# Gate and up of the last FFN as seven block products, and RWKV's row-group pairs in alternating order

## The chip, the cores and the metric

The kernel runs on one core of one Trainium2 chip. The metric is the device time of one execution in microseconds (us). A core has five engines that each run their own queue in order: PE (matrix products, 128 x 128 array, results in PSUM), DVE (vector operations), ACT (activations and copies), POOL and SP (here above all the issue of DMAs). PSUM has eight banks; a tile of 128 x 512 float32 numbers fills one.

## The reference

A trunk of two layers over 1024 tokens and 1024 features in float32, each layer a mixer and a SwiGLU FFN, with RMS norms before each and at the end. Layer 0 mixes with pooling and a Mamba-2 scan, layer 1 with RWKV-7 and RG-LRU.

```python
def swiglu(h, w_gate, w_up, w_down):
    return (jax.nn.silu(h @ w_gate) * (h @ w_up)) @ w_down

def reference(x, ...):
    h = x
    for layer in range(2):
        hn = rmsnorm(h, mix_norm_g[layer])
        mix = even_mixer(hn, ...) if layer % 2 == 0 else odd_mixer(hn, ...)
        h = h + mix
        hn = rmsnorm(h, ffn_norm_g[layer])
        h = h + swiglu(hn, ffn_w_gate[layer], ffn_w_up[layer], ffn_w_down[layer])
    return rmsnorm(h, final_norm_g)
```

`w_gate` and `w_up` are 1024 x 2816, `w_down` is 2816 x 1024. In RWKV-7 each of 8 heads has 64 channels, and two heads share the 128 rows of a tile.

## The kernel before, in words

The 1024 tokens are worked in two halves of 512 (`hf` 0 and 1, residuals `hA` and `hB`). Residuals lie transposed, features on the 128 partitions and 512 tokens along the free dimension, as 8 tiles. Float32 precision comes from splits: each operand is a high part (`hi`, an ACT cast to fp32r) and a low part (`lo`, DVE: source minus `hi`; `split`, lines 226 to 229, and for weights `wblock`, lines 341 and 342), and a product is three matmuls, high x high, high x low, low x high (`dense`, lines 363 to 365), each 128 rows deep with 512 moving columns.

An FFN half (`ffn`) takes F = 2816 as 22 blocks of 128, in 11 pairs. For a pair `gate_up` computes `pg` and `pu` (2 blocks x 8 k x 3 matmuls each), with tanh on ACT (line 493) and two products on DVE (494, 503) between; the result is split into `acth` and `actl`. Groups of pairs then go through `down`, four pairs of `py` tiles that are added into `h` (line 515). Of the last group in layer 1 `ffn_final` computes the down product with tokens on the partitions: `pf` holds the transposed residual (line 557) plus the products (lines 566 to 568, 256 columns); ACT squares and sums it (`fsq`, 570), a chain of small DVE operations gives the inverse root (`fst`, 572, 573, 214 to 218), and `xo` (577) is stored. `pg`, `pu`, `py` of `down`, and `pf` of the first two of four token tiles come from one pool of four PSUM banks (tag `pd`); the other four banks are a pool for everything else (`psum`).

The last FFN, `t.ffn(1, 1, hB, hn)`, follows the FFN of half 0 of the same layer, whose last pair calls `norm_apply` for `hB` beside it (line 297 on DVE, line 295 partly on POOL).

In the RWKV part `ps_A` (line 1156) are products of 64 rows: for each of 8 chunks and 4 head pairs, one matmul on the upper and one on the lower 64 rows of the array, into two PSUM tiles.

Weights are loaded into `raw` (3 buffers), their parts lie in `whi` and `wlo` (4 each). Other shared tags: `tf` (3), `sg` (2), `st` (3), `m` (28), `h` (8). The order of the instructions on each engine is set when the program is built, by a scheduler with its own simulation of time (`schedule_with_timeline_sim=True`); it keeps data dependencies and may otherwise mix work that the code issues one after the other. On the chip each engine keeps the order it was given.

Of the kernel before, what the change touches and what calls it, by code (L numbers as in the profile page):

```python
# [86 lines left out]
class Trunk:  # L87
# [453 lines left out]
    def ffn_final(self, hf, wd, base, act, h):  # L541

        nc = self.nc
        n = len(act)
        grep = [self.m2("grep") for _ in range(2)]
        for q in range(2):
            nc.sync.dma_start(grep[q], self.i["final_norm_g"][q * 512:(q + 1) * 512].rearrange("(o n) -> o n", o=1).broadcast_to([P, 512]))
        pair = lambda: [self.op.tile([P, 2, 256], F32R, name=x, tag="m", bufs=BUFS["m"]) for x in ("fh", "fl")]
        blk = []
        for m in range(4):  # L550
            blk.append(self.wblock(wd[base * P:(base + n) * P, m * 256:(m + 1) * 256], n, 256, pair))
        for c in range(4):
# [7 lines left out]
            for q in range(2):  # L560
                for k in range(n):
                    xh, xl = act[k]
                    for m in range(2):
                        wh, wl = blk[2 * q + m][k]
# [15 lines left out]
            self.tick()  # L580
            yield


# [324 lines left out]

    def odd_open(self, pool):
        nc, i = self.nc, self.i  # L910
        self.op = pool
        lng = pool.tile([P, H], F32, name="lng")
# [36 lines left out]
    def in1(self, hf, hn):  # L949
        nc, w = self.nc, self.i["od_w_in"][0]  # L950
        st = {}
# [5 lines left out]

        lw = self.op.tile([P, 2, 4, P], F32, name="lw", tag="m4", bufs=2)
        nc.gpsimd.memset(lw, 0.0)
# [89 lines left out]
    def rwkv(self, hf, st):  # L1049
        nc, op = self.nc, self.op  # L1050
        wdad, gd, r, k, v = st["wdad"], st["gd"], st["r"], st["k"], st["v"]
        TP = lambda n, shape, b=1: op.tile(shape, F32, name=n, tag=n, bufs=b)
        c64 = lambda a: a.rearrange("p (c t) -> p c t", c=8)
# [96 lines left out]
        for c in range(8):  # L1150
            am = op.tile([P, 4, 2, P], F32, name="am", tag="m4", bufs=2)
            pAs = [self.psum("ps_A") for _ in range(2)]
            for j in range(4):
# [11 lines left out]
        A = op.tile([P, 32, 32], F32, name="A", tag="m4", bufs=2)  # L1165
# [4 lines left out]
        X = op.tile([P, 32, 32], F32, name="X", tag="m4", bufs=2)  # L1170
        Xf = X.rearrange("p a b -> p (a b)")
# [20 lines left out]
        def prep1(c):  # L1192

            q, cc = c // 4, c % 4
            e = ch[c] = {}
            w1 = op.tile([P, 8, P], F32, name="w1", tag="m4", bufs=2)
            nc.sync.dma_start(w1, w1d[c])
# [124 lines left out]
    def gn(self, hf, c, y, v, bon, gd):  # L1322
# [6 lines left out]
        def part1():  # L1329
            s = op.tile([P, 4, 8], F32, name="gs", tag="gs", bufs=2)  # L1330
            mean, x, rs, t = (s[:, k, :] for k in range(4))
# [95 lines left out]
def trunk(tc, ins, out):  # L1427
    with ExitStack() as stack:
# [41 lines left out]
        t.later(2, lambda: rstd("B", stB))  # L1470
        with tc.tile_pool(name="op", bufs=1) as op:
            t.odd_open(op)
            hn2 = []
# [26 lines left out]
            t.flush()  # L1500
            run_all(t.ffn(1, 1, hB, hn))

# [27 lines left out]
```

## Time and profile before

| | |
|---|---|
| median of 3 runs | 2448.47 us (2446.02 to 2450.08) |
| profiled execution | 2448.01 us, of which the span of the trace is 2446.0 |
| PE busy | 2402.2 us (98%) |
| DVE busy | 1543.6 us (63%) |
| ACT busy | 911.6 us (37%) |
| POOL busy | 252.2 us (10%) |
| last FFN on PE | from 2065.3 us to the end |

Busy time counts each engine's instructions; a matmul's record is longer than the distance to the next one, since matmuls overlap, so the cost of one in a row is the distance between two starts, or the busy time of a window through the number of matmuls in it. The granted PE clock is given as a share of 2.4 GHz. A releaser in brackets is the instruction that ended the idle time before a row.

### The profile page before, as it was taken

Reading aid. Unit: us, or ns where it says so; the run is one execution under the profiler, and the core shown is the slowest. Engines: PE = TensorE matmul, PEld = TensorE weight load, DVE = VectorE, ACT = ScalarE, POOL = GpSimd, SP = SyncE. Lnnn points to the kernel's source line nnn. Section 1 sums busy time; section 2 is a strip of 40 time slices with the busy share of each in tenths; the row PEclk is TensorE's granted clock in tenths of the full one; section 3 lists DMA queues with packets and bytes.
Section 4 is the critical chain, followed back from the end, with each engine's and each line's share of the span. In section 5 each row is a group of like instructions: output and inputs, shape, how many; then the busy total and the mean of one; then the engine's idle time right before and its main releaser. Section 6 shows DMA issues by size and latency. Waiting matters only on the chain.

```text
span 2446.0 us, 33120 instructions
## 1 busy us (share of the span) xinstructions
PE 2402.2 (98%) x12323; PEld 1967.5 (80%) x12323; DVE 1543.6 (63%) x3052; ACT 911.6 (37%) x1612; POOL 252.2 (10%) x235
## 2 busy tenths in 40 slices
PE   7999999999999999999999999999999999999998
PEld 6878888888878887788888888877888888888887
DVE  7878767764476675675565768576465547444445
ACT  4434433222244564233333446432333334222222
POOL 2132121211111011100000110020000001000000
PEclk9989999999999999999999999999999999999999
DMA  5433533333345333543324533344432433333332
GB/s 164 119 90 102 161 107 109 90 113 95 92 152 158 89 106 95 162 143 106 97 80 138 168 112 104 96 136 137 138 101 81 142 121 125 96 95 95 95 95 78
DMA packets 296401, 280.17 MB, mean 115 GB/s; under 512 B 46130, under 2 KB 273608, under 8 KB 296240
## 3 DMA queue, kind: packets, MB, share of 16 engines
q1 hardware_dynamic: 295408, 277.64, 38.7%
q8 instruction: 97, 1.59, 0.3%
q0 software_dynamic: 832, 0.41, 0.1%
q14 instruction: 64, 0.52, 0.1%
HBM read 247.51 MB, written 30.49 MB: 114 GB/s over the span
## 4 chain that ended last, share of the span: by engine, by line
PE 91%; DVE 4%; DMA 2%; issue 1%; SPq 1%; ACT 1%; POOL 0%; DVEq 0%; ACTq 0%; POOLq 0%
PE pg L363 7%; PE pg L364 7%; PE pg L365 7%; PE pu L363 6%; PE pu L364 6%; PE pu L365 6%; PE py L363 6%; PE py L364 6%; PE py L365 6%; PE pi L363 5%; PE pi L364 5%; PE pi L365 5%; PE po L363 2%; PE po L364 2%; PE po L365 2%; PE ps_g L1259 1%
## 5 line engine op out<-in xcount | busy, mean ns | idle before, releaser
L342 DVE TENSOR_TENSOR wlo<-raw,whi 128x512 fp32r<-128x512 f32 (+1 forms) x744 | 538.5, 726 | 512.7 <-ACT whi L341 502.6
L341 ACT CAST whi<-raw 128x512 fp32r<-128x512 f32 (+1 forms) x744 | 458.8, 619 | 1050.9 <-PE pu L364 303.6
L363 PE MATMUL pu<-hnh,whi 128*128 128x512 f32 x736 | 292.5, 398 | 0.0
L365 PE MATMUL pu<-hnh,wlo 128*128 128x512 f32 x736 | 291.9, 397 | 0.0
L364 PE MATMUL pu<-hnl,whi 128*128 128x512 f32 x736 | 291.6, 396 | 0.0
L363 PE MATMUL pg<-hnh,whi 128*128 128x512 f32 x704 | 281.5, 400 | 0.0
L364 PE MATMUL pg<-hnl,whi 128*128 128x512 f32 x704 | 278.8, 396 | 0.0
L365 PE MATMUL pg<-hnh,wlo 128*128 128x512 f32 x704 | 276.5, 394 | 0.0
L363 PE MATMUL py<-acth,whi 128*128 128x512 f32 x672 | 262.8, 402 | 4.9 <-DVE sg L503 3.4
L364 PE MATMUL py<-actl,whi 128*128 128x512 f32 x672 | 266.7, 397 | 0.0
L365 PE MATMUL py<-acth,wlo 128*128 128x512 f32 x672 | 265.8, 396 | 0.0
L363 PE MATMUL pi<-hnh,whi 128*128 128x512 f32 x512 | 204.6, 400 | 0.2
L364 PE MATMUL pi<-hnl,whi 128*128 128x512 f32 x512 | 203.3, 397 | 0.0
L365 PE MATMUL pi<-hnh,wlo 128*128 128x512 f32 x512 | 201.7, 396 | 0.0
L363 PEld LDWEIGHTS pu<-hnh,whi 128*128 128x128 f32 x736 | 138.4, 188 | 33.4 <-issue 2.2
L365 PEld LDWEIGHTS pu<-hnh,wlo 128*128 128x128 f32 x736 | 138.4, 188 | 33.3 <-issue 0.7
L364 PEld LDWEIGHTS pu<-hnl,whi 128*128 128x128 f32 x736 | 138.4, 188 | 31.0
L363 PEld LDWEIGHTS pg<-hnh,whi 128*128 128x128 f32 x704 | 132.4, 188 | 30.9
L365 PEld LDWEIGHTS pg<-hnh,wlo 128*128 128x128 f32 x704 | 132.4, 188 | 30.8
L364 PEld LDWEIGHTS pg<-hnl,whi 128*128 128x128 f32 x704 | 132.3, 188 | 30.3
L363 PEld LDWEIGHTS py<-acth,whi 128*128 128x128 f32 x672 | 127.1, 189 | 36.8 <-issue 3.0
L365 PEld LDWEIGHTS py<-acth,wlo 128*128 128x128 f32 x672 | 127.0, 189 | 29.6
(443 smaller groups left out, 3737.0 us busy)
## 6 DMA issues: line engine op xcount, KB each, us to landing
raw<-in_ffn_w_gate SPq DMA_DIRECT2D x88, 512.0 KB
raw<-in_ffn_w_up SPq DMA_DIRECT2D x88, 512.0 KB
raw<-in_ffn_w_down SPq DMA_DIRECT2D x64, 512.0 KB
raw<-in_od_w_in SPq DMA_DIRECT2D x44, 512.0 KB
raw<-in_ev_w_in SPq DMA_DIRECT2D x36, 512.0 KB
raw<-in_ffn_w_down SPq DMA_DIRECT2D x48, 256.0 KB
yraw<-yd SPq DMA_DIRECT2D x32, 256.0 KB
raw<-in_ev_w_out SPq DMA_DIRECT2D x16, 512.0 KB
```

What stands on the lines that cost most here:

```text
L341: nc.scalar.copy(hi[:, :m, :width], raw[:, k:k + m, :width])
L342: nc.vector.tensor_tensor(lo[:, :m, :width], raw[:, k:k + m, :width], hi[:, :m, :width].bitcast(F32), op=SUB)
L363: nc.tensor.matmul(o, wh[:, a:b], xh, start=st, stop=False)
L364: nc.tensor.matmul(o, wh[:, a:b], xl, start=False, stop=False)
L365: nc.tensor.matmul(o, wl[:, a:b], xh, start=False, stop=en)
L1259: nc.tensor.matmul(pg[:, hs], e["w1"][:, h, :], e["S"][:, hs], start=h == 0, stop=h == 7)
```

## The change

The last FFN's gate and up products are replaced. For each block of 128 columns of F the two weight matrices and the two halves of the normalised input form a 2 x 2 block product: gate over the upper (`a11`) and lower (`a12`) 512 features, up likewise (`a21`, `a22`), against tokens left and right (`b11` to `b22`, 256 columns each). Seven products of half the depth and 256 columns take the place of eight, with sums of the weights (`s1` to `s4`, four DVE operations a block) and of the input (`t1` to `t4`, once, in `stras_norm`), and sums of the results. Each product is 4 k x 3 matmuls. `stras_norm` takes the place of `norm_apply` for `hB`. The down products of four blocks are spread over the blocks that follow, one pair of `py` tiles after each block from the fifth on, from the other PSUM pool. `ffn_final` keeps `grep` and its weights in other tags. In RWKV each `ps_A` matmul is told to come after the one before it, upper and lower rows in turn. Some RWKV tiles move to a pool `oq` that closes before the last FFN, which makes room for the pool `sp`.

```diff
+    def after(self, a, b):
+        if a is not None:
+            self.tc.add_manual_dep(b.ins, a.ins.name, mybir.DependencyInfo(mybir.DependencyClass.NoSync, mybir.DependencyReason.DATA),
+                                   reason="pairs of row groups")
+        return b
...
-        grep = [self.m2("grep") for _ in range(2)]
+        grep = [self.dp.tile([P, H], F32, name="grep", tag="st", bufs=BUFS["st"]) for _ in range(2)]
...
-        pair = lambda: [self.op.tile([P, 2, 256], F32R, name=x, tag="m", bufs=BUFS["m"]) for x in ("fh", "fl")]
...
-            blk.append(self.wblock(wd[base * P:(base + n) * P, m * 256:(m + 1) * 256], n, 256, pair))
+            blk.append(self.wblock(wd[base * P:(base + n) * P, m * 256:(m + 1) * 256], n, 256))
...
+    def stras_norm(self, X, h, r, gname, goff):
+        nc = self.nc
+        for k in range(4):
+            f, s = [], []
+            for j in (k, k + 4):
+                hn = self.dp.tile([P, H], F32, name="hn", tag="tf", bufs=BUFS["tf"])
+                nc.vector.scalar_tensor_tensor(hn, h[j], self.pv(gname, goff + j), r(), op0=MULT, op1=MULT)
+                hl = self.hn_tiles(j)
+                self.split(hn, *hl)
...
+            (b11, b12), (b21, b22) = [(x[:, :256], x[:, 256:]) for x in f]
...
+            nc.vector.tensor_tensor(t1, b12, b11, op=SUB)
+            nc.vector.tensor_tensor(t2, b22, t1, op=SUB)
+            nc.vector.tensor_tensor(t3, b22, b12, op=SUB)
+            nc.vector.tensor_tensor(t4, b21, t2, op=SUB)
+            for q in range(2):
+                self.split(ts[q], hi[q], lo[q])
...
+    def stras_weights(self, f, wg, wu):
...
+        for w in (wg, wu):
+            raw = self.dp.tile([P, 4, WB], F32, name="raw", tag="raw", bufs=BUFS["raw"])
+            raw = raw.rearrange("p k n -> p (k n)")[:, :1024]
+            nc.sync.dma_start(raw.rearrange("p (k n) -> p k n", k=8), w[:, f * P:(f + 1) * P].rearrange("(k p) n -> p k n", p=P))
+            raws.append(raw)
+        (a11, a12), (a21, a22) = [(x[:, :512], x[:, 512:]) for x in raws]
...
+        W["a11"], W["a12"] = two(raws[0])
+        W["a22"] = one(a22, *((self.dp, "nrb", 2) if f % 2 else (self.dp, "h", BUFS["h"])))
+        nc.vector.tensor_tensor(a22, a21, a22, op=ADD)
+        nc.vector.tensor_tensor(a21, a11, a21, op=SUB)
+        W["s3"], W["s1"] = two(raws[1])
+        nc.vector.tensor_tensor(a11, a22, a11, op=SUB)
+        W["s2"] = one(a11, self.op, "m", BUFS["m"])
+        nc.vector.tensor_tensor(a12, a12, a11, op=SUB)
+        W["s4"] = one(a12, self.op, "m", BUFS["m"])
+        return W
...
+    def stras_mm(self, o, a, b, first):
+        mm = self.nc.tensor.matmul
+        ah, al = a
+        for k in range(4):
+            c = slice(k * P, (k + 1) * P)
+            bh, bl = b[k]
+            mm(o, ah[:, c], bh, start=first and k == 0, stop=False, skip_group_check=True)
+            mm(o, ah[:, c], bl, start=False, stop=False, skip_group_check=True)
+            mm(o, al[:, c], bh, start=False, stop=k == 3, skip_group_check=True)
...
+        def finish(e):
+            Y, W, g, c22, n = e
+            self.stras_mm(Y[:, L], W["a22"], X["t4"], False)
+            nc.vector.scalar_tensor_tensor(g[:, L], g[:, L], 0.5, Y[:, L], op0=MULT, op1=MULT)
+            nc.vector.scalar_tensor_tensor(g[:, R], g[:, R], 0.5, c22, op0=MULT, op1=MULT)
...
+            self.split(g, *hl)
+            acts.append(hl)
...
+        for n in range(NFF):
+            W = self.stras_weights(n, wg, wu)
+            Y, Z = self.pd("py1"), self.pd("pz1")
+            self.stras_mm(Y[:, L], W["a11"], X["b11"], True)
+            rr = self.dp.tile([P, H], F32, name="rr", tag="st", bufs=BUFS["st"])
+            nc.scalar.copy(rr[:, L], Y[:, L])
+            self.stras_mm(Z[:, R], W["s1"], X["t1"], True)
+            c22 = self.dp.tile([P, H], F32, name="c22", tag="tf", bufs=BUFS["tf"])[:, :256]
+            nc.scalar.copy(c22, Z[:, R])
+            if prev:
+                finish(prev)
+            self.stras_mm(Y[:, L], W["s2"], X["t2"], False)
+            nc.scalar.copy(rr[:, R], Y[:, L])
+            self.stras_mm(Z[:, L], W["a12"], X["b21"], False)
+            self.stras_mm(Z[:, R], W["s4"], X["b22"], False)
+            g = self.dp.tile([P, H], F32, name="sg", tag="sg", bufs=BUFS["sg"])
+            nc.vector.tensor_tensor(g, rr, Z, op=ADD)
+            th = self.dp.tile([P, H], F32, name="th", tag="tf", bufs=BUFS["tf"])
+            nc.scalar.activation(th, g, AF.Tanh, scale=0.5)
+            nc.vector.scalar_tensor_tensor(g, th, 1.0, g, op0=ADD, op1=MULT)
+            self.stras_mm(Y[:, L], W["s3"], X["t3"], False)
+            nc.vector.tensor_tensor(c22, c22, Y[:, L], op=ADD)
+            prev = (Y, W, g, c22, n)
+            yield
+            if n % 4 == 0 and n:
+                todo = down(n - 4, acts[-4:])
+            if todo:
+                next(todo)
+                yield
...
-                    nc.tensor.matmul(pAs[b][:, j * P:(j + 1) * P], kb[j][c // 4][rows, c % 4, :], zr[j][c // 4][rows, c % 4, :],
-                                     start=True, stop=True)
+                    last = self.after(last, nc.tensor.matmul(pAs[b][:, j * P:(j + 1) * P], kb[j][c // 4][rows, c % 4, :],
+                                                             zr[j][c // 4][rows, c % 4, :], start=True, stop=True))
...
-            f = t.ffn(0, 1, hA, hn2, t.norm_apply(hn, hB, lambda: R["B"], "ffn_norm_g", 8))
+            f = t.ffn(0, 1, hA, hn2, t.stras_norm(X, hB, lambda: R["B"], "ffn_norm_g", 8))
...
-            run_all(t.ffn(1, 1, hB, hn))
+            late.close()
+            with tc.tile_pool(name="sp", bufs=1) as t.sp:
+                run_all(t.stras_ffn(1, 1, hB, X))
```

The order on the engines at three places. First PE where the last FFN begins; before, the last `pf` matmuls and the first of `pg` (brackets: what an instruction waits for on other queues):

```order
L566 MATMUL pf<-fh,acth 128x256
L567 MATMUL pf<-fl,acth 128x256
L568 MATMUL pf<-fh,actl 128x256
L363 MATMUL pg<-hnh_17977,whi 128x512 [waits DVE_49,Activation_49]
L364 MATMUL pg<-hnl_17978,whi 128x512
L365 MATMUL pg<-hnh_17977,wlo 128x512
L363 MATMUL pg<-hnh_17977,whi 128x512 [waits DVE_49]
```

After, the same place, the first product into `Y` (`py_...`), twelve matmuls of it, and the first into `Z` (`pz_...`):

```order
L572 MATMUL pf<-whi,acth 128x256
L573 MATMUL pf<-wlo,acth 128x256
L574 MATMUL pf<-whi,actl 128x256
L663 MATMUL py_18495<-hnh_17981,wah 128x256 [waits DVE_49,DMAHW0_49,PE_49,DMAHW1_49,Activation_49,Pool_49]
L664 MATMUL py_18495<-hnl_17982,wah 128x256
L665 MATMUL py_18495<-hnh_17981,wal 128x256
...
L665 MATMUL py_18495<-hnh_18093,wal 128x256
L663 MATMUL pz_18496<-th,wah 128x256 [waits DVE_49,Activation_49]
```

The first matmul of the stage now waits on every queue, among them that of DVE's `xo`, POOL and ACT; `Y` and `Z` are of the PSUM pool of which the first two token tiles' `pf` hold all four banks.

Second DVE around the first `xo`, before: the `fst` chain of a token tile stands in one piece and `xo` right behind it.

```order
L217 TENSOR_SCALAR fst<-fst 128x1 [waits DVE_49]
L218 SCALAR_TENSOR_TENSOR fst<-fst 128x1 [waits DVE_49]
L572 TENSOR_TENSOR fst<-fst 128x1 [waits Activation_49]
L577 SCALAR_TENSOR_TENSOR xo<-pf,fst,grep 128x512 [waits DVE_49,PE_49]
L577 SCALAR_TENSOR_TENSOR xo<-pf,fst,grep 128x512 [waits PE_49]
```

After, the rows up to the first `xo` (`raw` are the sums of weights, here of the second block):

```order
L224 TENSOR_SCALAR fst<-fst 128x1 [waits DVE_49]
L225 SCALAR_TENSOR_TENSOR fst<-fst 128x1 [waits DVE_49]
L649 TENSOR_TENSOR raw<-raw 128x512 [waits DVE_49]
L225 SCALAR_TENSOR_TENSOR fst<-fst 128x1 [waits DVE_49]
L224 TENSOR_SCALAR fst<-fst 128x1 [waits DVE_49]
L651 TENSOR_TENSOR raw<-raw 128x512 [waits DVE_49]
L224 TENSOR_SCALAR fst<-fst 128x1 [waits DVE_49]
L225 SCALAR_TENSOR_TENSOR fst<-fst 128x1 [waits DVE_49]
L653 TENSOR_TENSOR raw<-raw 128x512 [waits DVE_49]
L225 SCALAR_TENSOR_TENSOR fst<-fst 128x1 [waits DVE_49]
L583 SCALAR_TENSOR_TENSOR xo<-pf,fst,grep 128x512 [waits DVE_49]
L583 SCALAR_TENSOR_TENSOR xo<-pf,fst,grep 128x512 [waits PE_49]
```

The chain of `fst` and the first `xo` now stand behind and between operations on the weights of the first two blocks.

Third PE in RWKV, a chunk's `ps_A` products of one half; the two numbers of the tile are the two row groups. Before:

```order
L1156 MATMUL ps_A_9075<-zr_8568,kb_8570 128x128
L1156 MATMUL ps_A_9075<-zr_8649,kb_8651 128x128
L1156 MATMUL ps_A_9075<-zr_8720,kb_8722 128x128
L1156 MATMUL ps_A_9076<-zr_8568,kb_8570 128x128
L1156 MATMUL ps_A_9076<-zr_8649,kb_8651 128x128
L1156 MATMUL ps_A_9076<-zr_8720,kb_8722 128x128
L1156 MATMUL ps_A_9075<-zr_8757,kb_8759 128x128
L1156 MATMUL ps_A_9076<-zr_8757,kb_8759 128x128
```

After:

```order
L1305 MATMUL ps_A_9063<-zr_8652,kb_8654 128x128
L1305 MATMUL ps_A_9064<-zr_8652,kb_8654 128x128
L1305 MATMUL ps_A_9063<-zr_8723,kb_8725 128x128
L1305 MATMUL ps_A_9064<-zr_8723,kb_8725 128x128
L1305 MATMUL ps_A_9063<-zr_8760,kb_8762 128x128
L1305 MATMUL ps_A_9064<-zr_8760,kb_8762 128x128
L1305 MATMUL ps_A_9078<-zr_8571,kb_8573 128x128
L1305 MATMUL ps_A_9079<-zr_8571,kb_8573 128x128
```

Before, three of one tile stand in a row; afterwards the two tiles of a chunk take turns. At the first half's other chunks some stood in turns before too.

## Rows read from the trace of the kernel before

**Rows 1.** The page, busy time by engine, and the chain that ended last by engine

```profile
PE 2402.2 (98%) x12323; PEld 1967.5 (80%) x12323; DVE 1543.6 (63%) x3052; ACT 911.6 (37%) x1612; POOL 252.2 (10%) x235
...
PE 91%; DVE 4%; DMA 2%; issue 1%; SPq 1%; ACT 1%; POOL 0%; DVEq 0%; ACTq 0%; POOLq 0%
```

**Rows 2.** Busy time by window: us, busy (x instructions) per engine, PEclk, DMA share, GB/s

```profile
2064.00:2417.00 353.00, 353.00 (x1528) 286.14 (x1528) 162.86 (x262) 103.11 (x176) 0.00 (x0) 1.00 0.32 96
2417.00:2446.00 29.00, 19.87 (x149) 18.54 (x147) 15.93 (x54) 5.48 (x16) 0.00 (x0) 0.90 0.19 73
```

**Rows 3.** Groups by shape, PE, 2064 to 2417: busy us, mean ns | idle

```profile
L363 PE MATMUL pg<-hnh,whi 128*128 128x512 f32 x176 | 69.4, 394 | 0.0
```

**Rows 4.** Timeline of PE, tile pz of the first layer: start us, us, instruction

```profile
93.80 0.28 PE L718 MATMUL pz<-wlo,hnh 128*128 128x256 f32 x1
...
98.97 0.28 PE L717 MATMUL pz<-whi,hnh 128*128 128x256 f32 x1
```

**Rows 5.** Timeline of PE where the last FFN begins

```profile
2040.94 0.47 PE L363 MATMUL py<-acth,whi 128*128 128x512 f32 x1 [1.41 <-DVE sg L503]
...
2044.60 0.47 PE L363 MATMUL py<-acth,whi 128*128 128x512 f32 x1 [0.63 <-DVE h L515]
...
2065.14 0.28 PE L568 MATMUL pf<-fh,actl 128*128 128x256 f32 x1
2065.26 0.39 PE L363 MATMUL pg<-hnh,whi 128*128 128x512 f32 x1
```

**Rows 6.** Timeline of DVE, same place; in brackets idle before and what ended it

```profile
2025.54 1.90 DVE L297 SCALAR_TENSOR_TENSOR hn<-hB,par,nrb 128x512 f32<-128x512 f32 x1 [0.20 <-ACT nrb L272]
...
2029.17 0.74 DVE L297 SCALAR_TENSOR_TENSOR hn<-hB,par,nrb 128x512 f32<-128x512 f32 x1
2029.83 1.80 DVE L342 TENSOR_TENSOR wlo<-raw,whi 128x512 fp32r<-128x512 f32 x1
...
2043.78 0.68 DVE L515 TENSOR_TENSOR h<-h,py 128x512 f32<-128x512 f32 x1
2044.38 0.68 DVE L229 TENSOR_TENSOR actl<-sg,acth 128x512 fp32r<-128x512 f32 x1
...
2057.61 0.16 DVE L572 TENSOR_TENSOR fst<-fst 128x1 f32<-128x1 f32 x1 [3.44 <-ACT fsq L570]
2057.81 0.15 DVE L573 TENSOR_SCALAR fst<-fst 128x1 f32<-128x1 f32 x1
2057.99 0.15 DVE L214 TENSOR_SCALAR fst<-fst 128x1 int32<-128x1 int32 x1
...
2060.59 1.41 DVE L577 SCALAR_TENSOR_TENSOR xo<-pf,fst,grep 128x512 f32<-128x512 f32 x2
...
2077.47 0.69 DVE L494 SCALAR_TENSOR_TENSOR sg<-th,pg 128x512 f32<-128x512 f32 x1 [2.57 <-DMA out<-xo]
```

**Rows 7.** Busy time by window around a pause of PE

```profile
165.00:170.00 5.00, 1.67 (x3) 0.50 (x2) 4.92 (x14) 4.02 (x10) 1.06 (x1) 0.71 0.49 144
170.00:175.00 5.00, 2.30 (x10) 1.83 (x10) 4.82 (x11) 1.37 (x3) 2.12 (x2) 0.50 0.01 2
175.00:180.00 5.00, 5.00 (x16) 3.86 (x16) 4.19 (x10) 0.63 (x1) 1.93 (x2) 0.50 0.67 154
180.00:185.00 5.00, 5.00 (x22) 4.00 (x21) 3.40 (x10) 1.68 (x3) 1.18 (x2) 0.92 0.45 117
```

**Rows 8.** Operations on tile pz, PEld, ACT and DVE: ns min/median/max

```profile
L717 PEld LDWEIGHTS pz<-whi,hnh x128: 186/188/193, 93.5 to 275.5; 128*128 128x128 f32 x128
...
L693 ACT ACTIVATE zth<-pz x8: 369/380/385, 26.1 to 246.4; 128x256 f32<-128x256 f32 x8
L694 DVE SCALAR_TENSOR_TENSOR z<-zth,pz x8: 401/421/422, 26.5 to 247.3; 128x256 f32<-128x256 f32 x8
```

**Rows 9.** Groups by shape, ACT, 2070 to 2400

```profile
L341 ACT CAST whi<-raw 128x512 fp32r<-128x512 f32 x119 | 73.9, 621 | 218.0 <-PE pu L364 81.2 <-PE py L364 66.8 <-PE pg L364 58.2
```

**Rows 10.** Timeline of PE, the RWKV products ps_A

```profile
1012.35 1.16 PE L1156 MATMUL ps_A<-zr,kb 64*128 64x128 f32 x8
...
1015.04 1.17 PE L1156 MATMUL ps_A<-zr,kb 64*128 64x128 f32 x16
```

More of the change, by code (lines that the diff above doesn't have):

```diff
@@ L563, in ffn_final @@
                     for m in range(2):
-                        wh, wl = blk[2 * q + m][k]
+                        wh, wl = [x[:, :256] for x in blk[2 * q + m][k]]
                         o = ps[q][:, m * 256:(m + 1) * 256]
@@ L581, in ffn_final @@
             yield
+    def stras_norm(self, X, h, r, gname, goff):
[7 more added lines that the diff above has]
+                self.split(hn, *hl)
+                f.append(hn)
+                s.append(hl)
+                if j < 4:
+                    yield
+            (b11, b12), (b21, b22) = [(x[:, :256], x[:, 256:]) for x in f]
+            lo = [self.op.tile([P, H], F32R, name="tl", tag="m", bufs=BUFS["m"]) for _ in range(2)]
+            hi = [self.op.tile([P, H], F32R, name="th", tag="m", bufs=BUFS["m"]) for _ in range(2)]
+            ts = [self.m2("ts") for _ in range(2)]
+            t1, t2, t3, t4 = [x[:, q * 256:(q + 1) * 256] for x in ts for q in range(2)]
+            nc.vector.tensor_tensor(t1, b12, b11, op=SUB)
[4 more added lines that the diff above has]
+                self.split(ts[q], hi[q], lo[q])
+            L, R = slice(0, 256), slice(256, 512)
+            for b, (x, c) in dict(b11=(s[0], L), b21=(s[1], L), b22=(s[1], R), t1=((hi[0], lo[0]), L), t2=((hi[0], lo[0]), R),
+                                  t3=((hi[1], lo[1]), L), t4=((hi[1], lo[1]), R)).items():
+                X.setdefault(b, []).append([y[:, c] for y in x])
+            yield
@@ new lines, in stras_weights, with two, one @@
+    def stras_weights(self, f, wg, wu):
+        nc = self.nc
+        raws = []
+        for w in (wg, wu):
[4 more added lines that the diff above has]
+        (a11, a12), (a21, a22) = [(x[:, :512], x[:, 512:]) for x in raws]
+        C = slice(0, 512), slice(512, 1024)
+        def two(src):
+            hi, lo = [self.sp.tile([P, 1024], F32R, name=x, tag="ws", bufs=6) for x in ("wah", "wal")]
+            self.split(src, hi, lo)
+            return [(hi[:, c], lo[:, c]) for c in C]
+        def one(src, pool, tag, bufs):
+            hl = [pool.tile([P, 512], F32R, name=x, tag=tag, bufs=bufs) for x in ("wbh", "wbl")]
+            self.split(src, *hl)
+            return hl
+        W = {}
+        W["a11"], W["a12"] = two(raws[0])
[8 more added lines that the diff above has]
+        return W
@@ new lines, in stras_mm, with stras_ffn, down @@
+    def stras_mm(self, o, a, b, first):
[7 more added lines that the diff above has]
+            mm(o, al[:, c], bh, start=False, stop=k == 3, skip_group_check=True)
+    def stras_ffn(self, hf, layer, h, X):
+        nc, i = self.nc, self.i
+        wg, wu, wd = i["ffn_w_gate"][layer], i["ffn_w_up"][layer], i["ffn_w_down"][layer]
+        L, R = slice(0, 256), slice(256, 512)
+        acts = []
+        def finish(e):
[3 more added lines that the diff above has]
+            nc.vector.scalar_tensor_tensor(g[:, R], g[:, R], 0.5, c22, op0=MULT, op1=MULT)
+            if n % 8 < 5:
+                hl = self.act_tiles()
+            else:
+                hl = [self.dp.tile([P, H], F32R, name=x, tag="h", bufs=BUFS["h"]) for x in ("acth", "actl")]
+            self.split(g, *hl)
+            acts.append(hl)
+        def down(base, act):
+            for m in range(4):
+                pp = [self.psum("py"), self.psum("py")]
+                for _ in self.dense(wd, base, len(act), m * 256, 256, act, pp):
+                    pass
+                for t in range(2):
+                    nc.vector.tensor_tensor(h[2 * m + t], h[2 * m + t], pp[t], op=ADD)
+                yield
+        prev = None
+        todo = None
+        for n in range(NFF):
[21 more added lines that the diff above has]
+            prev = (Y, W, g, c22, n)
+            yield
+            if n % 4 == 0 and n:
+                todo = down(n - 4, acts[-4:])
+            if todo:
+                next(todo)
+                yield
+        finish(prev)
+        yield from todo
+        yield from self.ffn_final(hf, wd, NFF - 2, acts[-2:], h)
@@ L906, in ssd_unit, with odd_open @@
         yield
[L909 removed]
+    def odd_open(self, keep, pool):
         nc, i = self.nc, self.i
[L911 removed]
+        self.op, self.oq = keep, pool
         lng = pool.tile([P, H], F32, name="lng")
@@ L956, in proj @@
             return pp
-        lw = self.op.tile([P, 2, 4, P], F32, name="lw", tag="m4", bufs=2)
+        lw = self.oq.tile([P, 2, 4, P], F32, name="lw", tag="m4", bufs=2)
         nc.gpsimd.memset(lw, 0.0)
@@ L1150, in rwkv @@
         for c in range(8):
-            am = op.tile([P, 4, 2, P], F32, name="am", tag="m4", bufs=2)
+            am = self.oq.tile([P, 4, 2, P], F32, name="am", tag="m4", bufs=2)
             pAs = [self.psum("ps_A") for _ in range(2)]
+            last = None
             for j in range(4):
@@ L1164, in rwkv @@
             yield
-        A = op.tile([P, 32, 32], F32, name="A", tag="m4", bufs=2)
+        A = self.oq.tile([P, 32, 32], F32, name="A", tag="m4", bufs=2)
         for q in range(2):
@@ L1195, in prep1 @@
             e = ch[c] = {}
-            w1 = op.tile([P, 8, P], F32, name="w1", tag="m4", bufs=2)
+            w1 = self.oq.tile([P, 8, P], F32, name="w1", tag="m4", bufs=2)
             nc.sync.dma_start(w1, w1d[c])
@@ L1329, in part1 @@
         def part1():
-            s = op.tile([P, 4, 8], F32, name="gs", tag="gs", bufs=2)
+            s = self.oq.tile([P, 4, 8], F32, name="gs", tag="gs", bufs=2)
             mean, x, rs, t = (s[:, k, :] for k in range(4))
@@ L1470, in trunk @@
         t.later(2, lambda: rstd("B", stB))
-        with tc.tile_pool(name="op", bufs=1) as op:
-            t.odd_open(op)
+        with tc.tile_pool(name="op", bufs=1) as op, ExitStack() as late:
+            t.odd_open(op, late.enter_context(tc.tile_pool(name="oq", bufs=1)))
             hn2 = []
```

5 lines of the change are left out of this document (3 added, 2 removed).

## The prediction

> **What bounds the kernel now.** I read the page's shares and chain first: PE is busy for 2402.2 us of the span, and 91% of the chain that ended last is PE [rows 1]. Time is won by giving PE less to do, and lost where PE has to wait for another engine. The change is nearly all in the last FFN, so I then asked for the engines' busy time there. From 2064 to 2417 us PE is busy without a break, 353.00 us for 1528 matmuls, at full clock, so one 512-column matmul costs 353.00/1528 = 0.231 us; DVE has only 162.86 us of work, ACT 103.11, and the DMA queues 32% [rows 2]. The reader is to see two things: that this stretch is pure PE time, and that DVE has a lot of room on average. The groups of instructions give the gate and up matmuls: six kinds (three lines, `pg` and `pu`) of 176 each, 1056 in all [rows 3]. Last I read the two engines in order of time where the stage begins, because the first products need PSUM tiles that the FFN before still holds [rows 5, 6].
>
> **PE's work.** The 1056 gate and up matmuls go: 1056 x 0.231 = 243.9 us. In come 22 blocks x 7 products x 12 = 1848 matmuls with 256 moving columns. Such a matmul stands in two places before: in the first layer 45 in a row start 0.1175 us apart (the rows at 93.80 and 98.97 are the first and the last of them, 44 steps), and the `pf` rows 0.12 us apart [rows 4, 5]. I take 0.119, so 219.9 us, and the saving is **-24.0 us** (at 0.1175: -26.7; at 0.12: -22.1). The 480 down matmuls stay.
>
> The weight load of a 256-column matmul lasts 188 ns [rows 8], longer than the step of 0.1175 us, yet the steps are that short: the loads lie beside the matmuls and each other. The Trainium skill, "TensorE: Matmul & The Clock Gate", section "Back-to-back issue gap", speaks against the change: it says that in a stream of weight loads and matmuls both set the spacing, and that a matmul of a quarter of the columns costs 81 ns where a full one costs 131. By an estimate from that page, 256 columns would cost about three quarters of 512, and the change would add some 76 us. This case's rows give 0.1175 to 0.231, very nearly half, so the trace disagrees.
>
> **The start of the last FFN.** The first Strassen sums need two `pd` tiles; the FFN before gives them up with its first `xo`. Before, `pg` takes the same tiles, but PE runs from the last `pf` matmul into `pg` at 2065.26 without a gap [rows 5], since the first two `xo` read them at 2060.59 already [rows 6]. Afterwards the first product waits for DVE (first fence of PE's order), and DVE issues in order. What it has to do from the first normalisation row at 2025.54 [rows 6] to the first `xo` is counted in its new order: 22 operations of the old FFN (adds of `h`, low halves of weights, gates) and 16 splits and 8 normalisations of `stras_norm` with its 16 sums of 256 columns, then for blocks 0 and 1 eight sums, four splits of 512 and three of 1024 columns, and 20 small ones of the `fst` chain. In a row a 512-column operation takes 0.60 us (2043.78 to 2044.38), a normalisation 0.66 (2029.17 to 2029.83), a small one 0.19 [rows 6]. A 256-column one lasts 0.42 against 0.68 [rows 8], so 0.34 in a row, and 1024 columns by the same slope 1.13. The sum is 13.2 + 9.6 + 5.3 + 5.4 + 4.8 + 2.4 + 3.4 + 3.8 = 47.9 us. 2025.5 + 47.9 = 2073.4, and with the `xo` itself (0.75) the first tile is free at about 2074.3. Before, DVE was full from 2030 to 2050 too, partly since POOL's share of the normalisation stretched single operations to 1.8 us [rows 6]; that goes. So PE starts the stage at 2074.3 in place of 2065.26: **+9.0 us**. That PE no longer waits 1.41 and 0.63 us at 2040.94 and 2044.60 [rows 5] only makes it wait longer here, so it counts nothing. From below: if DVE gets ahead (it idled 3.44 us at 2057.61 before), the cost is 0; from above, with waits for ACT and the loads in that row, 16.
>
> After such a pause PE's clock falls. Between 165 and 175 us PE was idle for 6 us; it came back at half clock, 1.2 GHz, and was at full clock only after 180 [rows 7]. With PE busy again at some 173, that is 8 us at half clock, a loss of 4 us, of which DVE's lag hides a part: **+2.5 us** (0 to 5).
>
> **The first blocks.** Up to block 4 there is no down product, so a block is 84 x 0.119 = 10.0 us of PE. DVE has for a block: four sums (2.4), two splits of 1024 and three of 512 (4.1), `g`, its product and `c22` (1.5), `finish` (1.3): 9.3 us. It starts behind, with seven `xo` and their chains still queued, and each `xo` can wait for the output tile's store (2.57 us at 2077.47 [rows 6]). The two engines are level, so any wait of DVE shows on PE: **+3 us** (0 to 8, the 8 being two blocks in which DVE needs 4 us longer).
>
> **The steady blocks.** From block 4 on each block has 24 down matmuls too: 10.0 + 24 x 0.231 = 15.5 us of PE. DVE has 9.3 + 2.4 (two low halves, two adds into `hB`) = 11.7 us, and ACT some 7 us of the same casts as before (621 ns each [rows 9]) and three copies. Within a block the closest waits are those between two products in one half of a PSUM tile: 24 matmuls (2.8 us) lie between the product and the one that needs its copy, and the copy itself is 0.38 us [rows 8]. ACT's queue ahead of it can hold a cast of about 1.1 us. That holds, but not by much: **+1 us** (0 to 10, at half a microsecond in each of 18 blocks).
>
> **The end** changes `grep`'s and the weights' tiles; PE is busy for 19.87 of the last 29 us [rows 2], and the last block's chain is as long as before: **+0.5** (0 to 2). The loads are rows of 512 bytes in place of 1 KB with the same total, at a DMA share of 32%: nothing.
>
> **The RWKV pairs.** Eight 64-row matmuls in a row on one row group take 1.16 us by the records, sixteen that alternate take 1.17 [rows 10]: a pair costs what one costs, 0.112 us. In the order before, 22 of 32 pairs per half already alternate; afterwards 28 do. Two records per matmul and two halves: (84 - 72) x 0.112 x 2 = -2.7 us. Against it the new order is interrupted by other matmuls some eight times more, at about 0.2 us each (the first step of a run is 0.1 longer on either side): **-1 us** (-4.5, if all alternate in unbroken runs, to +1).
>
> Sum: -24.0 + 9.0 + 2.5 + 3 + 1 + 0.5 - 1 = -9.0. The profiled run took 2448.01 us (its span and 2.0 around it), 0.5 under the median of 2448.47. **Forecast: 2439 us.**
>
> **Rivals.** (1) The start hides: the scheduler's order is only an order, and DVE reaches the first `xo` as PE does. For it: DVE's 3.44 us of idle time at 2057.61. Against it: 47.9 us of work stand ahead of `xo`, and PE needs under 40 from the same moment (2025.54 to 2065.26). Then the 9.0 and 2.5 and most of the 3 go: about 2426. (2) Slower: DVE becomes the bound of the Strassen blocks. Its queue is in order, and a product's copy, the sums and the splits of two blocks stand in one row; an operation that waits for PE holds the splits that PE needs next. PE would then stall once in each steady block. From 0.5 us per block over 18 blocks (9 us) on nothing is gained; at 0.8 to 1.2 us, 14 to 22 us, the time is 2453 to 2460. For it: DVE at 11.7 of 15.5 us, 75%, against 46% before (162.86 of 353 us [rows 2]). Against it: the weights are a block ahead. (3) The weight load bounds 256-column matmuls: 1848 x 0.188 = 347 us against 243.9, +103, about 2550 with the rest. Against it: the step of 0.1175 us beside those loads [rows 4, 8]. (4) The pairs in RWKV bring the whole 4.5 us: 2435.5.
>
> **Chances.** My own sum, with 5 to 13 us for the start: 0.47 (2434 to 2445). Rival 1: 0.16. Rival 2: 0.22. Rival 3: 0.02. Rival 4: 0.07. Between the sum and rival 2, where losses eat up most of the gain: 0.06. About 0.2% (4.9 us) is what a measurement can tell from no change here, so same is 2443.6 to 2453.4. Same takes 0.07 of my own sum, that 0.06 and 0.04 of rival 2: 0.17. Slower takes the other 0.18 of rival 2 and rival 3: 0.20. Faster: 0.63. The range reaches from rival 1 into rival 2 and leaves out about 0.2: 2427 to 2455.
>
> **What the profile would show.** PE from the first Strassen product to the last down in 256-column steps of 0.12 us at full clock; an idle PE of some 10 us around 2064 to 2074, ended by `xo`, and half clock for some 5 us behind it; DVE busy without a break from 2030 to 2090; PE busy nearly throughout from block 5 on. I am wrong if the pause at the start is under 3 us or over 16, if PE's idle time inside the steady blocks sums to over 6 us, or if the 256-column step is not about 0.12.

## The result, and the profile after

The changed kernel takes 2427.4 us (median of 4 runs, 2426.6 to 2428.8) against 2447.9 for the kernel before: 20.5 us less, a ratio of 0.9917 (95% interval 0.9899 to 0.9934). The direction was forecast; the gain is more than twice the 9 us that were. 2427.4 lies 0.4 us above the lower end of the range. The profiled run has a span of 2425.9 us, 20.1 less than before, and the trace says where they are.

PE in the changed kernel, where the last FFN begins and where its down products end (start, duration, instruction; idle before it in brackets):

```profile
2057.44 0.28 PE L574 MATMUL pf<-whi,actl 128*128 128x256 f32 x1
2068.68 0.55 PE L663 MATMUL py<-hnh,wah 128*128 128x256 f32 x1 [10.96 <-DVE xo L583]
2069.03 0.41 PE L664 MATMUL py<-hnl,wah 128*128 128x256 f32 x1
2069.25 0.41 PE L665 MATMUL py<-hnh,wal 128*128 128x256 f32 x1
...
2091.02 0.28 PE L663 MATMUL py<-hnh,wah 128*128 128x256 f32 x1
2091.14 0.28 PE L664 MATMUL py<-hnl,wah 128*128 128x256 f32 x1
...
2401.48 0.39 PE L372 MATMUL py<-acth,wlo 128*128 128x512 f32 x1
```

The counterpart of the last row in the kernel before:

```profile
2421.79 0.39 PE L365 MATMUL py<-acth,wlo 128*128 128x512 f32 x1
```

Before, 1536 matmuls of 512 columns lie between 2065.26 [rows 5] and 2421.79, so one costs 356.5/1535 = 0.232 us. Afterwards the 256-column ones start 0.12 us apart; over the 1737 steps between two of them behind 2080 us the mean is 0.1185. The first ones, at 2069, are 0.22 apart: half clock.

The first product waits 10.96 us for `xo`. The same stretch by engines (busy us with counts for PE, weight loads, DVE, ACT, POOL; then the granted clock, DMA share, GB/s):

```profile
2040.00:2060.00 20.00, 17.72 (x140) 16.87 (x138) 19.96 (x42) 12.54 (x23) 0.00 (x0) 1.00 0.30 89
2060.00:2070.00 10.00, 1.32 (x6) 1.35 (x7) 8.27 (x23) 1.65 (x4) 0.00 (x0) 0.55 0.44 134
2070.00:2080.00 10.00, 10.00 (x69) 10.00 (x69) 7.74 (x27) 4.47 (x12) 0.00 (x0) 0.77 0.33 126
2080.00:2090.00 10.00, 10.00 (x86) 10.00 (x86) 8.19 (x14) 4.93 (x8) 0.00 (x0) 1.00 0.54 159
2110.00:2390.00 280.00, 280.00 (x1955) 261.04 (x1954) 221.40 (x346) 126.78 (x218) 0.00 (x0) 1.00 0.35 104
```

DVE is full up to 2060 and PE idle from 2058 to 2068.7; from there to the last down product PE has no gap at all, with DVE at 79% between 2110 and 2390 (221.40 of 280 us; 46% before [rows 2]). DVE's row from the first normalisation to the first `xo`:

```profile
2020.50 1.41 DVE L598 SCALAR_TENSOR_TENSOR hn<-hB,par,nrb 128x512 f32<-128x512 f32 x2 [0.20 <-ACT nrb L279]
...
2067.53 1.41 DVE L583 SCALAR_TENSOR_TENSOR xo<-pf,fst,grep 128x512 f32<-128x512 f32 x2
```

It takes 47.0 us; 47.9 were counted. But it begins at 2020.50, where it began at 2025.54 before [rows 6]: the program is 5.0 us ahead by then. The two traces part in RWKV. The `ps_A` runs of the second half afterwards:

```profile
1647.15 2.05 PE L1305 MATMUL ps_A<-zr,kb 64*128 64x128 f32 x30
1651.43 0.49 PE L1305 MATMUL ps_A<-zr,kb 64*128 64x128 f32 x2
1652.73 2.05 PE L1305 MATMUL ps_A<-zr,kb 64*128 64x128 f32 x30
```

and before:

```profile
1647.54 2.60 PE L1156 MATMUL ps_A<-zr,kb 64*128 64x128 f32 x32
1650.96 1.16 PE L1156 MATMUL ps_A<-zr,kb 64*128 64x128 f32 x8
...
1655.18 1.75 PE L1156 MATMUL ps_A<-zr,kb 64*128 64x128 f32 x16 [0.38 <-DVE am L1159]
...
1659.15 3.27 PE L1156 MATMUL ps_A<-zr,kb 64*128 64x128 f32 x32
```

Summed from each run's first row to the next other instruction, `ps_A` holds PE for 13.8 and 12.8 us in the two halves before and 11.1 and 10.9 afterwards: 4.6 us less.

| term | forecast | measured |
|---|---|---|
| seven products in place of eight | -24.0 | -26.3 (1848 x 0.1185 - 1056 x 0.2323) |
| start of the last FFN | +9.0 | +8.5 (2068.68 - 2065.26, and the 5.0 us of head start used up) |
| half clock | +2.5 | +2.6 (27 steps of 0.213 in place of 0.1185) |
| first blocks | +3 | 0 |
| steady blocks | +1 | 0 |
| end | +0.5 | +0.2 |
| before the last FFN | -1 | -5.0 |
| sum | -9.0 | -20.0 |

### The profile page after: what moved, and what is told of

Its sections match the earlier page's. It is cut to its first block, busy times and chain, and to the rows that moved or that the text cites. A ratio compares the mean times of both kernels' runs of the same rounds, so it can differ in the third digit from the quotient of the medians.

```text
span 2425.9 us, 34902 instructions
## 1 busy us (share of the span) xinstructions
PE 2373.9 (98%) x13115; PEld 1986.4 (82%) x13115; DVE 1656.8 (68%) x3248; ACT 966.5 (40%) x1708; POOL 244.0 (10%) x231
## 4 chain that ended last, share of the span: by engine, by line
PE 91%; DVE 4%; DMA 2%; issue 1%; SPq 1%; ACT 1%; POOL 0%; DVEq 0%; ACTq 0%; POOLq 0%
PE py L370 6%; PE py L371 6%; PE py L372 6%; PE pg L371 5%; PE pg L372 5%; PE pg L370 5%; PE pu L370 5%; PE pu L371 5%; PE pu L372 5%; PE pi L370 4%; PE pi L371 4%; PE pi L372 4%; PE po L370 2%; PE po L371 2%; PE po L372 2%; PE py L663 2%
## 5 line engine op out<-in xcount | busy, mean ns | idle before, releaser
L348 ACT CAST whi<-raw 128x512 fp32r<-128x512 f32 (+1 forms) x664 | 407.6, 619 | 877.8 <-PE pu L371 207.9
L349 DVE TENSOR_TENSOR wlo<-raw,whi 128x512 fp32r<-128x512 f32 (+1 forms) x664 | 477.6, 723 | 401.5 <-ACT whi L348 394.7
L370 PE MATMUL pu<-hnh,whi 128*128 128x512 f32 x560 | 223.5, 400 | 0.0
L371 PE MATMUL pu<-hnl,whi 128*128 128x512 f32 x560 | 223.1, 398 | 0.0
L372 PE MATMUL pu<-hnh,wlo 128*128 128x512 f32 x560 | 222.2, 397 | 0.0
L370 PE MATMUL pg<-hnh,whi 128*128 128x512 f32 x528 | 211.2, 400 | 0.0
L371 PE MATMUL pg<-hnl,whi 128*128 128x512 f32 x528 | 209.3, 396 | 0.0
L372 PE MATMUL pg<-hnh,wlo 128*128 128x512 f32 x528 | 208.4, 396 | 0.0
L371 PEld LDWEIGHTS py<-actl,whi 128*128 128x128 f32 x672 | 127.1, 189 | 27.3 <-DVE actl L236 0.2
L522 DVE TENSOR_TENSOR h<-h,py 128x512 f32<-128x512 f32 x160 | 107.6, 682 | 34.9 <-PE py L372 33.8
```

The source lines that it names most:

```text
L348: nc.scalar.copy(hi[:, :m, :width], raw[:, k:k + m, :width])
L349: nc.vector.tensor_tensor(lo[:, :m, :width], raw[:, k:k + m, :width], hi[:, :m, :width].bitcast(F32), op=SUB)
L370: nc.tensor.matmul(o, wh[:, a:b], xh, start=st, stop=False)
L371: nc.tensor.matmul(o, wh[:, a:b], xl, start=False, stop=False)
L372: nc.tensor.matmul(o, wl[:, a:b], xh, start=False, stop=en)
L522: nc.vector.tensor_tensor(h[f], h[f], pp[t], op=ADD)
```

## The experiments

Each ran beside the kernel before on its chip; where two of them are compared, their ratios to it are, and within the last FFN the traces, by the time from DVE's first normalisation row to the last down matmul (table below), which leaves out what comes ahead. Four traces with the same start (the changed kernel, `after_again`, `a_nopairs`, `a_dve4`) lie within 1.8 us in that time, so a smaller difference says nothing.

**Which part brings what.** `b_pairs` is the kernel before with the alternating order alone; `a_nopairs` the changed kernel without it; `b_runs` the kernel before with the opposite order.

```diff
 b_pairs:   last = self.after(last, nc.tensor.matmul(pAs[b]...))   # for j: for b:
 a_nopairs: nc.tensor.matmul(pAs[b]...)                            # as before
 b_runs:    last = self.after(last, nc.tensor.matmul(pAs[b]...))   # for b: for j:
```

> The kernel before with the alternating order of the ps_A products alone. In the changed kernel's trace PE is 5.0 us ahead of the kernel before when the work for the last FFN begins. If the alternation brings that by itself (theory A), this kernel is 4 to 5.5 us faster than before, about 2443. If most of the 5.0 us come from the other edits, by a differently shuffled order (theory B), it is 0 to 2.7 us faster, 2445 to 2448.

Measured: 5.2 us faster by the medians, 4.4 by the ratio (0.9982, 0.9973 to 0.9991, which is 2.2 to 6.6 us). Theory A.

> The changed kernel without the alternating order: the seven products alone. Theory A: 15 to 16 us faster than before, about 2432 (26.2 for the products, less 8.5 for the pause at the start and 2.6 for the clock). Theory B: 18 to 20 us faster, about 2428 to 2430, since the head start of 5 us stays for the most part.

Measured: 15.5 us faster (0.9937, 0.9925 to 0.9950), and in its trace DVE's normalisation begins at 2026.05, 0.5 us from the kernel before. The head start was the pairs. Its size is known to a few us only: in the nine other traces with the pairs DVE's normalisation begins between 2016.9 and 2020.7, 4.9 to 8.7 us ahead of the kernel before. By the medians the two parts add up: 5.2 + 15.5 = 20.7, against 20.5 measured together.

> The kernel before with the ps_A products held in the opposite order: four of one row group, then four of the other. By the records a pair costs as much as a single one, 0.112 us a pass; 22 of 32 pairs of each half would be lost: 22 x 2 passes x 0.112 x 2 halves = 10 us slower than before, about 2458 (theory A). If PE's time there is set by other engines, under 3 us slower.

Measured: 4.7 us slower by the medians, 6.4 by the ratio (1.0026, 1.0013 to 1.0040, which is 3.2 to 9.8 us). That is less than the 10 us, since the order that holds four of a group still left 23 of 44 record pairs per half (a matmul leaves two records) beside each other, where one group ends and the next begins: the 21 lost ones are 21 x 0.112 x 2 = 4.7 us. The executions spread from 2447.7 to 2465.0 us. The profiled one has a span of 2460.2 us, 14 more than before; about 10 of them are a stretch in the second half's `ps_A` at half clock, some 20 us long (windows as above; the clock is the third figure from the right; from 1665 to 1675 it was 0.54).

```profile
1645.00:1655.00 10.00, 10.00 (x53) 7.79 (x52) 5.72 (x12) 2.87 (x5) 2.35 (x1) 0.93 0.53 131
1655.00:1665.00 10.00, 10.00 (x44) 8.15 (x44) 3.61 (x6) 0.01 (x1) 0.00 (x0) 0.50 0.65 177
```

PE was busy throughout these windows; what made the clock fall is open.

**The pause.** My theory was that `xo`'s place in DVE's queue is the price of the start, since it holds the PSUM banks.

```diff
+                if hf == 0 and c < 2:
+                    pc = self.m2("pc")
+                    nc.scalar.copy(pc, ps[q])
+                    ps[q] = pc
```

> The changed kernel, in which ACT copies the first four pf tiles of half 0 to SBUF right behind fsq and xo reads the copy, so that the first products' PSUM banks come free without DVE. If the pause of 11.0 us comes from xo's place in DVE's queue (my theory), the pause and the half clock behind it go: 9 to 13 us less than the changed kernel, about 2416. Rival: the banks only hide that the split weights and the sums of the input are late too (DVE's queue is the same work); then the pause ends at most 2 to 5 us earlier, about 2423 to 2425, or comes back as waits in the first blocks.

Measured: 0.9928 (0.9915 to 0.9940), no gain on the changed kernel's 0.9917. The pause all but went (first product 38.4 us behind the first normalisation row, in place of 48.2), but PE then waits in the first blocks:

```profile
PE py L667 <- ACT rr L707: 3.1, 1, 3.1
PE py L667 <- ACT wbh L235: 2.9, 1, 2.9
PE py L667 <- issue: 1.2, 1, 1.2
```

The theory in that form fell. One reason could be that the copies hold `m` tiles, so the next two kernels put them elsewhere (`a_pfact`: tags `acth` and `actl`; `a_pfact2`: also `o = ps[q]`, so that `xo` is written over the copy). `after_again` is the changed kernel as their neighbour.

```diff
 a_pfact:  -pc = self.m2("pc")
           +pc = self.dp.tile([P, H], F32, name="pc", tag=("acth", "actl")[q], bufs=BUFS["act"])
 a_pfact2: +o = ps[q] if hf == 0 and c < 2 else self.dp.tile([P, H], F32, name="xo", tag="sg", bufs=BUFS["sg"])
```

> The changed kernel once more, as the neighbour of the two that follow on the same chip: about 20 us faster than before, as measured (ratio 0.9917).

Measured: 2425.4 us, 0.9920 (0.9907 to 0.9933).

> As a_pfcopy, with the four copies of pf in the tags acth and actl, which are free there, in place of the tag m. In the trace of a_pfcopy the pause went, but PE then stood still for 3.1 us behind ACT's rr and 2.9 behind wbh, and those behind xo: the copies held the m tiles that the split s2 and s4 of the first blocks need. If that is all (theory C), the pause goes and the waits don't come back: 8 to 11 us less than the changed kernel. If DVE's amount of work from the normalisation on is what sets the pace (theory D), PE starts early and waits later in the first blocks: within 3 us of the changed kernel.

> As a_pfact, and the first four xo are written over their copies, so that only four of eight xo go through the two sg buffers that block 0's gate waits for. Theory C: another 1 to 2 us less than a_pfact, since g of block 0 waited 1.2 us for xo's store. Theory D: no difference from a_pfact.

Measured: 0.9929 (0.9916 to 0.9943) and 0.9927 (0.9915 to 0.9939), both within the 3 us that theory D gave, if anything slower than their neighbour. In `a_pfact2` the waits have moved again, to DVE's own splits and to copies of ACT that stand behind operations waiting for DVE:

```profile
PE pz L672 <- DVE wal L236: 2.4, 1, 2.4
PE py L670 <- ACT rr L710: 2.3, 1, 2.3
PE pz L670 <- ACT wah L235: 1.1, 1, 1.1
```

The three kernels also give ACT four more copies of some 0.6 us each, and in `a_pfact2` ACT waits in the same stretch for a load of weights:

```profile
2062.58 0.62 ACT L235 CAST wbh<-raw 128x512 fp32r<-128x512 f32 x1 [1.89 <-DMA raw<-in_ffn_w_up]
```

In the changed kernel ACT waits 2.80 us for a load of the same matrix, but inside the pause. So the runs show that the held banks alone are not what the pause costs. That all the later waits come from DVE's amount of work (theory D) fits them, but ACT's copies and that load were not tested apart.

**Moving DVE's work, and taking some away.** `a_xofirst` lets four sums on block 1's weights stand only behind the first `xo`; `a_nosums` leaves the 16 sums of the input out; `a_batchpool` gives the sums to POOL and makes one chain of half 0's four `fst` chains.

```diff
 a_xofirst:   x = nc.vector.tensor_tensor(a22, a21, a22, op=ADD)
+             if f == 1: self.after(self.xo0, x)
 a_nosums:   -nc.vector.tensor_tensor(t1, b12, b11, op=SUB)   # and t2, t3, t4
 a_batchpool: nc.gpsimd.tensor_tensor(t1, b12, b11, op=SUB)   # and t2, t3, t4
```

> The changed kernel in which the four sums on the second block's weights may only stand behind half 0's first xo on DVE (order alone; the work is the same). They take about 0.65 us each in the row ahead of xo, so by my theory the first xo, the first product and the end come 2.6 us earlier: about 2424.8. Rival (the row ahead of xo isn't what holds PE): no change, 2427.4.

Measured: 0.9924 (0.9908 to 0.9941): the time doesn't show it. In the trace the first product is at 45.3 us in place of 47.7 to 48.2, and the last down product 0.8 to 2.6 us earlier than in the four traces with the same start; two waits, together 1.2 us, come back in the first blocks.

> The changed kernel without the 16 sums of the input (t1 to t4; the products then use the plain halves of the input in their place, everything else as it was). This takes 16 x 0.34 = 5.4 us out of DVE's row and puts nothing on another engine; in the new order the row ahead of the first xo is some 7.9 us shorter, the rest of it moved behind xo. Theory D (DVE's amount of work from the normalisation to the second block sets when the products are done): 5 to 8 us less than the changed kernel, and what was only moved behind xo brings nothing lasting, so nearer 5. Rival (only the row ahead of the first xo counts): 8 us and the half clock, up to 10. If neither: no change, and the pause is then filled by another wait.

Measured: 0.9906 (0.9890 to 0.9923), 3.4 us less than `after_again` by the ratios, though the two intervals overlap; in the trace the first product is 5.0 to 5.5 us earlier and the end 2.7 to 4.5. That is less than the 5 us expected, with the right sign. Against the mean of the four traces with the same start (379.9), the end comes 3.4 us earlier for 5.4 us of work taken off, and in `a_xofirst` 1.5 us earlier for 2.6 us of work moved: in proportion about as much, so these two runs don't show that taking work away helps and moving it doesn't.

> The changed kernel with less work for DVE between the normalisation and the first xo: the four chains of half 0's final norm are one chain of 13 operations on four columns (27 fewer), and the 16 sums of the input (t1 to t4) are done by POOL, which is idle there. The row ahead of the first xo is 5.4 (sums) and 1 us (chain) shorter. Theory D (DVE's amount of work sets the start): the first product starts 5 to 6 us earlier, and with a shorter pause the time falls by 5 to 7 us against the changed kernel, about 2419. Rival (POOL's operations stretch DVE's beside them, as hn's did in the kernel before, five times from 0.68 to 1.8 us): 16 sums stretch as many DVE operations, and the gain is under 2 us or a loss.

Measured: 0.9942 (0.9929 to 0.9956), 5.4 us slower than `after_again`: a loss, as the rival had it (in the kernel before four DVE operations had been stretched to 1.8 or 1.9 us, not five). DVE's operations beside POOL's, DVE first:

```profile
2024.32 1.22 DVE L349 TENSOR_TENSOR wlo<-raw,whi 128x512 fp32r<-128x512 f32 x1
2025.47 1.22 DVE L610 SCALAR_TENSOR_TENSOR hn<-hB,par,nrb 128x512 f32<-128x512 f32 x1
2026.61 0.68 DVE L236 TENSOR_TENSOR hnl<-hn,hnh 128x512 fp32r<-128x512 f32 x1
2027.21 1.22 DVE L236 TENSOR_TENSOR tl<-ts,th 128x512 fp32r<-128x512 f32 x1
```

```profile
2023.92 1.07 POOL L625 TENSOR_TENSOR ts<-hn,ts 128x256 f32<-128x256 f32 x1
2024.96 1.18 POOL L622 TENSOR_TENSOR ts<-hn 128x256 f32<-128x256 f32 x1
2026.83 1.05 POOL L624 TENSOR_TENSOR ts<-hn 128x256 f32<-128x256 f32 x1 [0.69 <-DVE hn L610]
```

Where the two overlap, a DVE operation of 512 columns takes 1.22 us in place of 0.68; eleven single ones do so, 11 x 0.54 = 5.9 us, more than the 5.4 us of sums that DVE was spared. Each stretched row above ends 0.55 us behind the POOL row that it overlaps; the one at 2026.61, which began before POOL's, kept its 0.68. PE felt it ahead of the last FFN, where the changed kernel's PE has no wait:

```profile
PE py L370 <- DVE sg L510: 5.6, 1, 5.6
```

The row to the first `xo` became 50.9 us long. But the run changes two things, and the single chain costs too: it needs all four token tiles and so begins only at 2065.68, 46.2 us behind the first normalisation row, with `xo` behind it.

```profile
2065.68 0.16 DVE L563 TENSOR_TENSOR fst<-fst 128x4 f32<-128x4 f32 x1
```

How the loss divides between POOL's sums and the chain was not tested.

**How much room DVE has in a steady block.** Blocks 6 to 19 compute the low part of `s4` four or eight times more.

```diff
+        if 6 <= f < 20:
+            for _ in range(4):      # a_dve8: 8
+                nc.vector.tensor_tensor(W["s4"][1], a12, W["s4"][0].bitcast(F32), op=SUB)
```

> The changed kernel with four more DVE operations of 512 columns (the low part of s4 computed again, the same values) in the weights of blocks 6 to 19: 14 x 4 x 0.60 = 33.6 us of DVE work. My reading of the trace: a block has 15.4 us of PE and about 12 us of DVE, so 14.4 still fit: 0 to 3 us slower, 2427 to 2430. Rival (waits between DVE and PE in a block are already tight): a good part of 33.6 us shows, over 10 us slower.

> The same with eight more operations a block, 67 us of DVE work: a block then has about 16.8 us of DVE against 15.4 of PE, so DVE bounds it: 14 x 1.4 = some 20 us slower, 2440 to 2455. If PE remains without a gap, my count of DVE's work in a block is too high.

Measured: 0.9920 (0.9904 to 0.9936) and 1.0081 (1.0066 to 1.0096). The same window as above, 2110 to 2390, first `a_dve4`, then `a_dve8`:

```profile
2110.00:2390.00 280.00, 280.00 (x1950) 260.80 (x1949) 248.88 (x397) 126.56 (x214) 0.00 (x0) 1.00 0.34 103
```

```profile
2110.00:2390.00 280.00, 257.87 (x1708) 233.76 (x1707) 249.34 (x401) 108.24 (x186) 0.00 (x0) 0.98 0.29 87
```

This window also holds blocks without the extra work. From 2200 to 2300 every block has it, again `a_dve4` and then `a_dve8`:

```profile
2200.00:2300.00 100.00, 100.00 (x702) 93.24 (x701) 92.27 (x148) 46.65 (x79) 0.00 (x0) 1.00 0.32 98
2200.00:2300.00 100.00, 88.30 (x587) 78.55 (x586) 90.79 (x146) 37.33 (x64) 0.00 (x0) 1.00 0.26 80
```

33.6 us of extra DVE work cost nothing: PE has no gap, with DVE at 92%. Another 33.6 cost 42 us (421.6 against 379.6 in the table), twice what I expected: DVE gets no further than 91%, while PE stands still for 11.7 of the 100 us, and over the longer window the granted clock is 0.98. PE's waits there are many and short, for DVE's low parts (`wal`, `wbl`) and for ACT's high ones (`wah`, `wbh`). That two queues in order which wait for each other lose the last tenth is my reading; no run tests it.

From the first normalisation row on DVE (0) to the first product on PE, the first `xo`, and the start of the last down matmul, read from the timeline of each trace, in us:

| kernel | first product | first xo | last down |
|---|---|---|---|
| changed kernel | 48.2 | 47.0 | 381.0 |
| after_again | 47.7 | 46.6 | 379.2 |
| a_nopairs | 47.8 | 46.7 | 379.8 |
| a_dve4 | 47.7 | 46.6 | 379.6 |
| a_xofirst | 45.3 | 44.2 | 378.4 |
| a_nosums | 42.7 | 41.6 | 376.5 |
| a_pfcopy | 38.4 | 44.2 | 383.3 |
| a_pfact | 37.1 | 45.7 | 382.8 |
| a_pfact2 | 37.1 | 45.8 | 380.9 |
| a_batchpool | 52.0 | 50.9 | 386.2 |
| a_dve8 | 47.7 | 46.6 | 421.6 |

A first product that starts 10 us earlier doesn't end the stage earlier (the three copies of `pf`); with 5.4 us less DVE work it ends 2.7 to 4.5 us earlier (`a_nosums`). No version that does all of the work is faster than the changed kernel beyond its uncertainty.

## Why the prediction was right in direction and short in size

- **The products.** Right in mechanism: the 256-column step is 0.1185, near the 0.1175 of the first layer's rows, with weight loads of 189 ns beside it, and the rival of the weight load is refuted. The size was 2.3 us short because the window of 353.00 us with its 1528 matmuls also holds twelve `pf` ones of 256 columns, up to 2065.26; the distance of two starts gives 0.232 for a 512-column matmul, not 0.231, and the 256-column step was 0.1185 and not 0.119.
- **The start.** Right, and nearly to the microsecond: the row of 47.9 us was 47.0, the pause 11.0, its net price 8.5 for 9.0. What it stands for was only half understood. I wrote of tiles that `xo` holds; the copies of `pf` show that freeing the tiles alone gains nothing. The sign that DVE would be busy without a break up to 2090 did not come either: from 2060 on it was busy for 8.27, 7.74 and 8.19 of each 10 us.
- **The clock.** 2.6 for 2.5; it was at half clock for 6 us behind the pause.
- **The first blocks** (+3) and **the steady blocks** (+1) are the steps that failed in the last FFN: both cost nothing. As I now read it, the first blocks' price and the pause are one debt of DVE's and I charged it twice: while PE stands still, DVE gets ahead with the weights of blocks 0 and 1, and PE finds them ready (no wait behind the first product). Where the pause was taken away the price came, as waits of PE and a longer half clock (`a_pfcopy`: 344.9 us from the first product to the last down, against 332.8), though ACT's copies may have a part in it. For the steady blocks, 11.7 us of DVE against 15.5 of PE was right within 0.6 (79%), and the four extra operations of `a_dve4` show that there were more than 2 us to spare, which I hadn't credited.
- **The RWKV pairs** (-1) are the step most wrong: -5.0. The gain of pairing was -2.7 by the records, to which I added 1.7 us of interruptions. The 2.7 was right: 56 of 64 record pairs per half stand beside each other afterwards, as counted, and `ps_A` holds PE for 4.6 us less in all. The 1.7 was the wrong term, in size and in sign. The order has 11 runs per half in place of 8, three more and not eight; and the long runs of before hid restarts and waits of their own (steps of 0.2 to 0.4 us inside the 3.27 us of the last run, and PE waiting 0.38 us for DVE's `am` at 1655.18), which the alternating order lost. My lower bound, -4.5, lies within half a microsecond of the trace; rival 4 had it, with a chance of 0.07.
- **Rivals.** Rival 1 forecast the time (2426) for a reason that didn't hold: the start did not hide. The range reached down to 2427 for its sake, so that the time lies just inside it is luck. Rival 2 would have needed more than 2.4 us of further DVE work per block (`a_dve4` has that much and no gap); `a_dve8` is what it looks like.

Of the 11.0 us that the forecast was short by the trace, 4.0 are the pairs, 4.0 the first and steady blocks, 2.3 the products, and 0.7 the start, the clock and the end.

## What to carry to other kernels

A pause of the bounding engine and the waits that one expects right behind it may be one and the same debt of the engine it waits for: count that engine's work from its first late instruction to the point where it has caught up, and charge it once. To see whether a held buffer or the work behind it is the cause, give the buffer free early: if the end doesn't move, the buffer alone was not it, and the work behind it is the next thing to vary. Vary one thing at a time: `a_batchpool` changed two and can't be divided. For row-group pairs, count the restarts and waits inside the old order's runs, not only the pairs.

## What the runs showed of the hardware

Two records of 64-row matmuls on different row groups cost one step of 0.112 us, as one does alone, and holding them in turns was worth 2.2 to 6.6 us (`b_pairs`) in a kernel where 44 of 64 pairs already stood side by side by chance. In `b_runs` PE's clock fell to half for some 20 us in a stretch with such matmuls although PE was busy (0.50 from 1655 to 1665). A POOL operation of 256 columns took 1.1 us and made a DVE operation of 512 columns beside it 1.22 us long in place of 0.68. The Trainium skill, "SBUF — State Buffer", section "SBUF: two separate sides", says that the two share one pair of ports, which whoever starts first holds for a whole instruction when DVE reads two operands from SBUF; the rows above agree: DVE's operation ends 0.55 us behind POOL's where POOL began first, and keeps its length where DVE did. In the steady blocks PE had no gap with DVE busy for 92% of the time; with still more DVE work DVE's share stayed at 91% and PE lost the time.
